# Three parts of x on ScalarE's DMA queue, and a new order in the opening of the first feed-forward block

## The chip, the cores and the metric

The kernel runs on one core of a Trainium2 chip. The metric is the device time of one execution in microseconds (us), the median of several runs; lower is better. The core has a matrix engine (TensorE, PE in the profile, with its weight loads as PEld), VectorE (DVE), ScalarE (ACT), GpSimd (POOL) and SyncE (SP), which here only issues DMAs. The engines run on their own and wait for each other by semaphores; each of them works through its instructions in the order of the program.

## What is computed

Two layers of a decoder trunk on x, 256 tokens by 1024 columns, in float32:

```python
for l in range(DEPTH):
    h = h + 0.5 * swiglu(rms_norm(h, ffn1_norm[l]), ffn1_w_gate[l], ffn1_w_up[l], ffn1_w_down[l])
    h = h + hybrid_mixer(rms_norm(h, mix_norm[l]), w_in[l], ...)
    h = h + 0.5 * swiglu(rms_norm(h, ffn2_norm[l]), ffn2_w_gate[l], ffn2_w_up[l], ffn2_w_down[l])

def swiglu(x, w_gate, w_up, w_down):
    return (jax.nn.silu(x @ w_gate) * (x @ w_up)) @ w_down
```

The change lies in the first feed-forward block of the first layer alone. There `x @ w_gate` and `x @ w_up` have an inner length of 1024 (eight tiles k of 128 rows) and 2816 columns (22 tiles f of 128).

## The kernel before

**Arithmetic.** TensorE multiplies in a reduced format, so every float32 operand is cut into a high and a low part: `wh` is a cast of the weight (a copy on ScalarE or GpSimd), `wl` is the weight minus `wh` (a subtraction on VectorE or GpSimd). The activation has the same two parts, `norm.h` and `norm.l`, which lie side by side as `norm.x`. A "wide" product is `wh` with `norm.x` (512 columns), a "narrow" one `wl` with `norm.h` (256 columns). Each gate or up tile of 128 columns takes eight of each, and `summed` then adds the two halves of the PSUM bank.

**Loads.** `Weights` streams 1 MB pieces into five raw buffers and hands out the split units (`high`, `low`, `take`, `pump`). All loads of weights go through SP. The opening is loaded by hand: `load_x(mp)` brings two of x's eight k tiles (256 KB) into `trunk`; `W.load(i, m)` brings part m of the first gate (i = 0) or up piece (i = 1). In this text x0 to x3 are the four parts of x, g0, g1 and u0, u1 the parts of the gate and up pieces with k tiles 0 and 1, and 2 and 3; g2 and u2 the parts with k tiles 4 to 7 (512 KB each). The next two pieces, for the tiles f of 2 and 3, come behind them. The completion of a DMA counts up one of eight semaphores, DMAHW0 to DMAHW7, which are dealt out in turn over all queues; a DMA that gets a semaphore again waits until the DMA that had it before has landed.

**The opening** (`opening`, and the lines after it up to the loop over f). PE turns x's parts by transposes against `ident` (L535), ScalarE copies the turned part out, scaled (L362, the high part), VectorE makes the low part (L365). With `opening`, the first two tiles f (pairs p0 and p1) are multiplied together, over k tiles 0 to 3 as x and the weights come in, then (`hi`) over k tiles 4 to 7. `warm_up` issues products of ones, whose result nobody reads: WARM ahead of the first transposes, BRIDGE behind them. `norm.sums` and `norm.broadcast` make the reciprocal root that `gated` multiplies in. Then the loop over f takes one gate and one up tile at a time; odd tiles are `swapped` (narrow products first), even ones have the wide products first; from f = 4 on a tile of the down projection (`down`) stands between.

Of the kernel before, what the change touches and what calls it, by code (L numbers as in the profile page):

```python
# [18 lines left out]
P = 128  # L19
S = 256  # L20
D = 1024
KT = D // P
# [131 lines left out]
def kernel(ctx: ExitStack, tc: tile.TileContext, x, ffn1_norm, ffn1_w_gate, ffn1_w_up, ffn1_w_down,  # L154
                      mix_norm, w_in, forget_bias, a_q_norm, a_k_norm, b_q_norm, b_k_norm, c_q_norm, c_k_norm,
                      w_out, ffn2_norm, ffn2_w_gate, ffn2_w_up, ffn2_w_down, const, out):
    nc = tc.nc
# [39 lines left out]
    def tmp(n):  # L197
        return tp.tile([P, 512], F32, name="tmp", tag="tmp")[:, :n]
# [22 lines left out]

    def load_x(mp):
        cols = slice(256 * mp, 256 * mp + 256)
        nc.sync.dma_start(trunk[:, :, cols], x[0].rearrange("(t p) d -> p t d", p=P)[:, :, cols])  # L224

    load_x(0)
    load_gains(rows, ffn1_norm, nc.scalar)
    A.activation(tmp(P), ones, AF.Exp)

    def head_gains(l):  # L230
        gb = at.tile([P, 4, HD], F32, name="gb", tag="sg")
# [7 lines left out]
    def add_ffn(wg, wu, wd, first=False):  # L239
        gsrc, usrc, dsrc = (w.rearrange("(k p) c -> p k c", p=P) for w in (wg, wu, wd))  # L240
        rid = {}

        def half(kind, i):
            j = i // 2
            if (kind, j) not in rid:
                if kind == "d":
                    rid[kind, j] = W.add_raw((2, D), [(np.s_[:], dsrc[:, 2 * j:2 * j + 2, :])])
                else:
                    src = gsrc if kind == "g" else usrc
                    src = src[:, :, 256 * j:256 * j + 256]  # L250
                    cuts = [np.s_[:]]
                    if first and j < 2:
                        cuts = ([np.s_[:, 0:2], np.s_[:, 2:4], np.s_[:, 4:8]],
                                [np.s_[:, :, 0:P], np.s_[:, :, P:2 * P]])[j]
                    rid[kind, j] = W.add_raw((KT, 256), [(c, src[c]) for c in cuts])
            o = i % 2
            if kind == "d":
                W.add_unit(rid[kind, j], lambda r, o=o: r[:, o:o + 1, :], D, 1)
            elif first and j == 0:
                W.add_unit(rid[kind, j], lambda r, o=o: r[:, 4 * o:4 * o + 4], D, 4)  # L260
            else:
                W.add_unit(rid[kind, j], lambda r, o=o: r[:, :, o * P:(o + 1) * P], D, KT)

        for f in range(NF):
            half("g", f)
            half("u", f)
            if f == NF - 1:
                half("d", f - 1 - DOWN_LAG)
            if DOWN_LAG <= f != NF - 2:
                half("d", f - DOWN_LAG)  # L270
        for k in range(NF - DOWN_LAG, NF):
            half("d", k)
# [22 lines left out]
    W.n_raw_done -= RAW_BUFS - 4  # L295
    W.issue()
    for m in range(2):
        if m:
            load_x(m)
        for i in range(2):  # L300
            W.load(i, m)
    for mp in range(2, 4):
        load_x(mp)
    for i in range(2):
        W.load(i, 2)
    load_gains(more_rows[0:16], mix_norm, nc.sync)
    load_gains(more_rows[16:32], ffn2_norm, nc.sync)
    for m in range(2):
# [28 lines left out]
    def mm(o, l, r, start, stop):  # L337
        T.matmul(o, l, r, start=start, stop=stop, skip_group_check=True)  # L338
# [82 lines left out]
    def ffn(norm, nxt, aside=None, first=False):  # L421
# [23 lines left out]
        class Pair:  # L445
# [3 lines left out]
                self.ws = ws or [[[v[:, k] for k in range(KT)] for v in W.take()] for _ in range(2)]  # L449
                self.ps = [bank("gu").rearrange("p (a b) -> p a b", a=2) for _ in range(2)]  # L450

            def wide(self, ks):
                for w, ps in zip(self.ws, self.ps):
                    for k in ks:
                        mm(ps, w[0][k], norm.x[:, k], k == 0, False)

            def narrow(self, ks):
                for w, ps in zip(self.ws, self.ps):
                    for k in ks:
                        mm(ps[:, 0], w[1][k], norm.h[:, k], False, k == KT - 1)  # L460

            def swapped(self, between):

# [6 lines left out]
                        mm(ps, w[0][k], norm.x[:, k], False, k == KT - 1)  # L470
                return self.ps

            def both(self, ks=range(KT)):
                self.wide(ks)
                self.narrow(ks)
                return self.ps

        def summed(ps):

            o = tmp(S)  # L480
            A.copy(o, ps[:, 1])  # L481
            V.tensor_tensor(o, ps[:, 0], o, op=ALU.add)  # L482
            return o
# [24 lines left out]
        def opening():  # L508

            low = [W.high_tiles() for _ in range(2)]  # L510
            p0, p1 = (Pair([[[v[:, k, f * P:(f + 1) * P] for k in range(4)] for v in (h, l)] for _, h, l in low])
                      for f in range(2))

            def split(i, m, high, E):

                src, h, l = low[i]
                ks = slice(2 * m, 2 * m + 2)
                high(h[:, ks], src[:, ks])
                E.tensor_tensor(l[:, ks], src[:, ks], h[:, ks].bitcast(F32), op=ALU.subtract)  # L519

            def wide(i, k):
                for p in (p0, p1):
                    mm(p.ps[i], p.ws[i][0][k], norm.x[:, k], k == 0, False)

            def narrow(i, k):
                for p in (p0, p1):
                    mm(p.ps[i][:, 0], p.ws[i][1][k], norm.h[:, k], False, False)

            def turn(mp):

                ps = []
                for m in (2 * mp, 2 * mp + 1):
                    ps.append(bank("acc")[:, :S])
                    for t in range(2):
                        T.transpose(ps[-1][:, t * P:(t + 1) * P], trunk[:, t, m * P:(m + 1) * P], ident)  # L535
                return ps

            def parts(mp, ps):
                for i in range(2):
                    norm.high(2 * mp + i, ps[i])  # L540
                for i in range(2):
                    norm.low(2 * mp + i, ps[i])

            def squares(c):
                for t in range(2):
                    norm.squares(t, c)

            xT = turn(0)
            warm_up(BRIDGE)
            for m in range(2):  # L550
                ks = (2 * m, 2 * m + 1)
                parts(m, xT)
                split(0, m, G.tensor_copy, V)
                split(1, m, A.copy, G)
                for k in ks:
                    wide(0, k)
                if m:
                    xT = turn(2)
                for k in ks:
                    narrow(0, k)  # L560
                if m:
                    squares(0)
                    parts(2, xT)
                xT = turn(2 * m + 1)
                for k in ks:
                    wide(1, k)
                for k in ks:
                    narrow(1, k)
            parts(3, xT)
            for _ in range(2):  # L570
                W.low_done()
                W.take()
            src, h, _ = W.high_tiles()
            G.tensor_copy(h, src)
            W.high()
            W.low()
            W.low()
            squares(1)
            high = [W.take() for _ in range(2)]
            for f, p in enumerate((p0, p1)):  # L580
                for w, u in zip(p.ws, high):
                    for part, v in zip(w, u):
                        part.extend(v[:, k, f * P:(f + 1) * P] for k in range(4))
            return p0, p1

        lo, hi = range(KT // 2), range(KT // 2, KT)
        if first:
            p0, p1 = opening()
# [5 lines left out]
            p1.both(lo)  # L594
        W.pump()
        norm.sums()
        (g0, u0), (g1, u1) = p0.both(hi), p1.ps
        W.pump()
        g0, u0 = summed(g0), summed(u0)
        W.pump()  # L600
        p1.wide(hi)
        norm.broadcast(first)
        p1.narrow(hi)
        W.pump()
        t_, th = gated(g0)
        if not first:
# [4 lines left out]
        for f in range(1, NF):  # L611
            last = f == NF - 1
            def lagging():
                if DOWN_LAG <= f != NF - 2:
                    down(f - DOWN_LAG - last)

            if f == 1:
                g, u = g1, u1
            elif f % 2:
                g, u = Pair().swapped(lagging)  # L620
            else:
                p = Pair()
                p.wide(range(KT))
                lagging()
                p.narrow(range(KT))
                g, u = p.ps
            if last:
                W.pump()
            low_first = first and f == 1
            g = summed(g)  # L630
            if low_first:
                W.low()
            if not last:
                u = summed(u)
            t_, th = gated(g)
            if last:
                W.low()
                down(f - DOWN_LAG)
            else:
                if low_first:  # L640
                    W.high()
                else:
                    W.pump()
                if f == 1:
                    lagging()
                if f >= DOWN_LAG:
                    W.pump()
            silu(t_, th)
            hidden(f, t_, th, summed(u) if last else u, 3 if last else 1 + (first and f in (2, 3)))
            if f == 4 and first:  # L650
                load_small()
            if f == 8 and aside:
                aside()
# [653 lines left out]
```

## Time and profile before

| what | value |
|---|---|
| median of 3 runs | 1009.53 us (1009.43 to 1010.38) |
| the profiled execution, its own time | 1009.91 us |
| its span (first to last instruction) | 1008.2 us |
| PE busy in the span | 1003.4 us (100%), 5724 matmuls |
| PEld, DVE, ACT, POOL busy | 857.9, 795.3, 588.2, 169.1 us |
| HBM traffic | 184 MB, 182 GB/s over the span |

A matmul's busy time contains the time in the pipeline, so rows of products that follow each other overlap: 16 wide products on end take 3.82 us, though each lasts 390 ns. The pace of a row of products is what counts, and a busy PE is not a sign of full pace.

### The profile page before, as it was taken

To read this page: it belongs to the slowest core of one execution; us is meant where nothing else is said; L and a number is where in the kernel's file an instruction comes from. 1 tells how busy PE (TensorE), PEld (TensorE's weight loads), DVE (VectorE), ACT (ScalarE), POOL (GpSimd) and SP (SyncE) were. 2 spreads that over 40 slices of the span, in tenths; PEclk is the share of its full clock that TensorE was granted. 3 is DMA by queue.
4 is the path that set the end of the run, shared out by engine and by line. 5 is a ranking of instruction groups with operands and counts; after the bars stand their busy time and mean duration, and the time that the engine had idled before them with its cause. 6 is when DMAs were issued, how large, how long until landed. Compare 5 with 4: busy or idle time off the path is not lost.

```text
span 1008.2 us, 15271 instructions
## 1 busy us (share of the span) xinstructions
PE 1003.4 (100%) x5724; PEld 857.9 (85%) x5724; DVE 795.3 (79%) x1466; ACT 588.2 (58%) x1078; POOL 169.1 (17%) x196
## 2 busy tenths in 40 slices
PE   9999999999999999999999999999999999999998
PEld 7888888888878888888888888888888788888887
DVE  5978778779988877777878777787899877777775
ACT  6555555567776555555465555556677765555552
POOL 2003000058732000000000030001776320000000
PEclk9999999999999999999999999999999999999999
DMA  9765647474624455655655655665556255474731
GB/s 287 265 215 165 224 153 238 138 244 168 225 89 168 149 185 170 206 181 202 203 168 172 209 185 190 201 192 176 180 205 230 68 180 172 130 244 136 242 126 42
DMA packets 133497, 184.60 MB, mean 183 GB/s; under 512 B 7152, under 2 KB 106928, under 8 KB 133424
## 3 DMA queue, kind: packets, MB, share of 16 engines
q1 hardware_dynamic: 133392, 183.62, 54.8%
q8 instruction: 45, 0.74, 0.3%
q14 instruction: 28, 0.23, 0.1%
q10 hardware_dynamic: 32, 0.01, 0.0%
HBM read 182.55 MB, written 1.06 MB: 182 GB/s over the span
## 4 chain that ended last, share of the span: by engine, by line
PE 98%; DMA 1%; SPq 0%; ACT 0%; issue 0%; DVE 0%
PE ps_gu L338 66%; PE ps_acc L338 30%; PE ps_acc L179 1%; PE ps_acc L373 1%; DMA raw<-in_ffn_w_up_dram 1%; PE ps_gu L179 1%; SPq L99 0%; SPq L224 0%; PE ps_acc L940 0%; ACT wh L125 0%; PE ps_acc L400 0%; PE ps_acc L875 0%; PE ps_acc L821 0%; DVE trunk L417 0%; PE ps_acc L402 0%
## 5 line engine op out<-in xcount | busy, mean ns | idle before, releaser
L129 DVE TENSOR_TENSOR wl<-raw,wh 128x1024 fp32r<-128x1024 f32 (+2 forms) x342 | 418.2, 1232 | 25.4 <-ACT wh L125 25.0
L125 ACT CAST wh<-raw 128x1024 fp32r<-128x1024 f32 (+2 forms) x341 | 342.2, 1036 | 24.3 <-PE ps_gu L338 13.9
L338 PE MATMUL ps_gu<-xhl,wh 128*128 128x512 f32 x1408 | 330.5, 390 | 0.5 <-ACT wh L125 0.5
L338 PEld LDWEIGHTS ps_gu<-xhl,wh 128*128 128x128 f32 x1408 | 262.7, 188 | 54.8 <-ACT wh L125 0.9
L338 PEld LDWEIGHTS ps_gu<-xhl,wl 128*128 128x128 f32 x1408 | 175.9, 191 | 4.1 <-DVE wl L519 0.2
L338 PE MATMUL ps_gu<-xhl,wl 128*128 128x256 f32 x1408 | 178.7, 283 | 0.0
L482 DVE TENSOR_TENSOR tmp<-ps_gu,tmp 128x256 f32<-128x256 f32 x176 | 72.9, 423 | 109.3 <-ACT tmp L481 108.8
L338 PE MATMUL ps_gu<-wh,xhl 128*128 128x512 f32 (+2 forms) x512 | 155.1, 378 | 0.0
L338 PE MATMUL ps_acc<-wh,hh 128*128 128x512 f32 (+1 forms) x352 | 137.2, 390 | 0.0
L338 PE MATMUL ps_acc<-wl,hh 128*128 128x512 f32 (+1 forms) x352 | 137.0, 389 | 0.0
L338 PE MATMUL ps_acc<-wh,hl 128*128 128x512 f32 (+1 forms) x352 | 136.5, 388 | 0.0
L481 ACT COPY tmp<-ps_gu 128x256 f32<-128x256 f32 x176 | 63.4, 371 | 92.1 <-PE ps_gu L338 91.9
L338 PEld LDWEIGHTS ps_gu<-wh,xhl 128*128 128x128 f32 x512 | 94.6, 188 | 16.8 <-issue 1.7
L496 ACT CAST hh<-tmp 128x256 fp32r<-128x256 f32 x80 | 32.6, 407 | 120.2 <-DVE tmp L493 120.2
L338 PE MATMUL ps_gu<-wl,xhl 128*128 128x512 f32 (+2 forms) x256 | 95.7, 374 | 0.0
L488 ACT ACTIVATE tmp<-tmp 128x256 f32<-128x256 f32 x88 | 36.9, 419 | 82.9 <-DVE tmp L486 82.8
L349 POOL TENSOR_TENSOR y_n<-msq,minus_half 128x2 f32<-128x2 f32 x6 | 7.0, 1174 | 440.9 <-DVE msq L348 440.9
L338 PEld LDWEIGHTS ps_acc<-wh,hl 128*128 128x128 f32 x352 | 66.1, 188 | 13.8
L338 PEld LDWEIGHTS ps_acc<-wh,hh 128*128 128x128 f32 x352 | 66.2, 188 | 12.6
L338 PEld LDWEIGHTS ps_acc<-wl,hh 128*128 128x128 f32 x352 | 66.3, 188 | 12.3 <-DVE wl L129 0.2
L338 PEld LDWEIGHTS ps_gu<-wl,xhl 128*128 128x128 f32 x256 | 48.2, 188 | 7.0
L493 DVE TENSOR_TENSOR tmp<-tmp 128x256 f32<-128x256 f32 x88 | 37.6, 427 | 3.0
(228 smaller groups left out, 903.7 us busy)
## 6 DMA issues: line engine op xcount, KB each, us to landing
raw<-in_ffn_w_down_dram SPq DMA_DIRECT2D x44, 1024.0 KB, 5.0
raw<-in_ffn_w_gate_dram SPq DMA_DIRECT2D x42, 1024.0 KB, 7.0
raw<-in_ffn_w_up_dram SPq DMA_DIRECT2D x42, 1024.0 KB, 7.9
raw<-in_w_in_dram SPq DMA_DIRECT2D x24, 1024.0 KB, 5.0
raw<-in_w_out_dram SPq DMA_DIRECT2D x8, 1024.0 KB, 5.0
raw<-in_w_in_dram SPq DMA_DIRECT2D x4, 768.0 KB, 4.8
raw<-in_w_in_dram SPq DMA_DIRECT2D x4, 656.0 KB, 4.0
raw<-in_ffn_w_gate_dram SPq DMA_DIRECT2D x3, 512.0 KB, 7.9
```

Of the source, the lines that this page charges most:

```text
L125: self.nc.scalar.copy(hv, src)
L129: (engine or self.nc.vector).tensor_tensor(lv, self.srcs[self.n_low], hv.bitcast(F32), op=ALU.subtract)
L179: T.transpose(b[:, 64 * i:64 * i + 64], src[r], ident[r, r])
L338: T.matmul(o, l, r, start=start, stop=stop, skip_group_check=True)
L349: G.tensor_tensor(y, dst, minus_half[:, :n], op=ALU.pow)
L373: T.transpose(ps[:, i, t * P:(t + 1) * P], trunk[:, t, (2 * mp + i) * P:(2 * mp + i + 1) * P], ident)
L481: A.copy(o, ps[:, 1])
L482: V.tensor_tensor(o, ps[:, 0], o, op=ALU.add)
L488: A.activation(th, t_, AF.Tanh, scale=0.5)
L493: V.tensor_tensor(t_, u, t_, op=ALU.mult)
L496: (V.tensor_copy if late else A.copy)(hh, t_)
```

## The change

It has six parts, all of them in the first feed-forward block of the first layer.

1. `load_x` issues x1, x2 and x3 on ScalarE's queue, and a loop right behind ScalarE's first activation calls it for these three. The call for x1 between the weights is taken out; the old loop for x2 and x3 below stays, so that these two are loaded a second time, to the same place, and on ScalarE's queue too.
2. g2 and u2 are cut into two parts of 256 KB each (here g2a, g2b, u2a, u2b).
3. GpSimd casts g2 in two halves, ScalarE u2 in two halves.
4. Over k tiles 4 to 7, the wide gate products of p0 and p1 stand first, then p0's narrow gate products and its up products; p1's narrow gate products come next.
5. Tile f = 3 has its wide products first.
6. For f = 1, both sums (`summed`) stand ahead of a low part (`W.low`).

```diff
 def load_x(mp):
-        nc.sync.dma_start(trunk[:, :, cols], x[0].rearrange("(t p) d -> p t d", p=P)[:, :, cols])
+        (nc.scalar if mp else nc.sync).dma_start(trunk[:, :, cols], x[0].rearrange("(t p) d -> p t d", p=P)[:, :, cols])

     load_x(0)
     load_gains(rows, ffn1_norm, nc.scalar)
     A.activation(tmp(P), ones, AF.Exp)
+    for mp in range(1, 4):
+        load_x(mp)
...
-                        cuts = ([np.s_[:, 0:2], np.s_[:, 2:4], np.s_[:, 4:8]],
+                        cuts = ([np.s_[:, 0:2], np.s_[:, 2:4], np.s_[:, 4:6], np.s_[:, 6:8]],
...
     for m in range(2):
-        if m:
-            load_x(m)
         for i in range(2):
             W.load(i, m)
     for mp in range(2, 4):
         load_x(mp)
     for i in range(2):
-        W.load(i, 2)
+        for m in (2, 3):
+            W.load(i, m)
...
-            src, h, _ = W.high_tiles()
-            G.tensor_copy(h, src)
-            W.high()
+            for copy in (G.tensor_copy, A.copy):
+                src, h, _ = W.high_tiles()
+                for ks in (slice(0, 2), slice(2, 4)):
+                    copy(h[:, ks], src[:, ks])
...
-        (g0, u0), (g1, u1) = p0.both(hi), p1.ps
+        if first:
+            p0.wide(hi, (0,))
+            p1.wide(hi, (0,))
+            p0.narrow(hi, (0,))
+            p0.both(hi, (1,))
+        else:
+            p0.both(hi)
+        (g0, u0), (g1, u1) = p0.ps, p1.ps
...
-        p1.wide(hi)
+        if first:
+            p1.narrow(hi, (0,))
+        p1.wide(hi, (1,) if first else (0, 1))
         norm.broadcast(first)
-        p1.narrow(hi)
+        p1.narrow(hi, (1,) if first else (0, 1))
...
-            elif f % 2:
+            elif f % 2 and not (first and f == 3):
                 g, u = Pair().swapped(lagging)
...
             g = summed(g)
+            if not last:
+                u = summed(u)
             if low_first:
                 W.low()
-            if not last:
-                u = summed(u)
```

Three places show how this moves the instructions. The first is ScalarE from the start of the program, before; tmp<-in_ffn_norm is the load of the gains, xhl the turned x, wh<-raw 128x512 the cast of u0:

```order
L208 DMA tmp<-in_ffn_norm_dram 16x128
L228 ACT_TABLE_LOAD
L228 ACTIVATE tmp<-ones 128x128 [waits Pool_49]
L362 ACTIVATE xhl<-ps_acc,gT 128x256 [waits DVE_49,PE_49]
L362 ACTIVATE xhl<-ps_acc,gT 128x256 [waits PE_49]
L518 CAST wh<-raw 128x512 [waits DMAHW3_49]
```

and the same place now:

```order
L208 DMA tmp<-in_ffn_norm_dram 16x128
L228 ACT_TABLE_LOAD
L228 ACTIVATE tmp<-ones 128x128 [waits Pool_49]
L224 DMA trunk<-in_x_dram 128x2x256 x2
L224 DMA trunk<-in_x_dram 128x2x256 [waits DMAHW0_49]
L224 DMA trunk<-in_x_dram 128x2x256 [waits DMAHW6_49,DMAHW3_49]
L224 DMA trunk<-in_x_dram 128x2x256 [waits DMAHW5_49,DMAHW0_49]
L363 ACTIVATE xhl<-ps_acc,gT 128x256 [waits DVE_49,PE_49]
L363 ACTIVATE xhl<-ps_acc,gT 128x256 [waits PE_49]
L518 CAST wh<-raw 128x512
```

Five loads of x (x1, x2, x3, and x2 and x3 again) now stand ahead of the first copy of the turned x. Counted in turn, DMAHW0 belongs first to the gains and then to x3, DMAHW3 to u0, DMAHW5 to g1, DMAHW6 to x2.

The second place is SP's queue from the start, before:

```order
L224 DMA trunk<-in_x_dram 128x2x256
L99 DMA raw<-in_ffn_w_gate_dram 128x2x256
L99 DMA raw<-in_ffn_w_up_dram 128x2x256
L224 DMA trunk<-in_x_dram 128x2x256
L99 DMA raw<-in_ffn_w_gate_dram 128x2x256
L99 DMA raw<-in_ffn_w_up_dram 128x2x256
L224 DMA trunk<-in_x_dram 128x2x256
L224 DMA trunk<-in_x_dram 128x2x256 [waits DMAHW0_49]
L99 DMA raw<-in_ffn_w_gate_dram 128x4x256 [waits DMAHW1_49]
L99 DMA raw<-in_ffn_w_up_dram 128x4x256 [waits DMAHW2_49]
```

and now:

```order
L224 DMA trunk<-in_x_dram 128x2x256
L99 DMA raw<-in_ffn_w_gate_dram 128x2x256
L99 DMA raw<-in_ffn_w_up_dram 128x2x256
L99 DMA raw<-in_ffn_w_gate_dram 128x2x256
L99 DMA raw<-in_ffn_w_up_dram 128x2x256
L99 DMA raw<-in_ffn_w_gate_dram 128x2x256 [waits DMAHW1_49]
L99 DMA raw<-in_ffn_w_gate_dram 128x2x256 [waits DMAHW2_49]
L99 DMA raw<-in_ffn_w_up_dram 128x2x256 [waits DMAHW4_49]
L99 DMA raw<-in_ffn_w_up_dram 128x2x256 [waits DMAHW6_49]
```

g1 and u1 stand one place earlier; u2a waits for x1 (DMAHW4) and u2b for x2 (DMAHW6).

The third place is TensorE over k tiles 4 to 7, before; gate banks are 158 (p0) and 160 (p1), up banks 159 and 161:

```order
L338 MATMUL ps_gu_158<-xhl_149,wh_249 128x512 x4
L338 MATMUL ps_gu_159<-xhl_149,wh_252 128x512 x4
L338 MATMUL ps_gu_158<-xhl_149,wl_250 128x256 x4
L338 MATMUL ps_gu_159<-xhl_149,wl_253 128x256 x4
L338 MATMUL ps_gu_160<-xhl_149,wh_249 128x512 x4
L338 MATMUL ps_gu_161<-xhl_149,wh_252 128x512 x4
```

and now, with gate banks 162 and 164, up banks 163 and 165:

```order
L339 MATMUL ps_gu_162<-xhl_153,wh_253 128x512 x4
L339 MATMUL ps_gu_164<-xhl_153,wh_253 128x512 x4
L339 MATMUL ps_gu_162<-xhl_153,wl_254 128x256 x4
L339 MATMUL ps_gu_163<-xhl_153,wh_257 128x512 x4
L339 MATMUL ps_gu_163<-xhl_153,wl_258 128x256 x4
L339 MATMUL ps_gu_164<-xhl_153,wl_254 128x256 x4
L339 MATMUL ps_gu_165<-xhl_153,wh_257 128x512 x4
```

The first product with the up weights (wh_252 before, wh_257 now) stands behind twelve products instead of four.

## Rows read from the trace of the kernel before

**Rows 1.** Four stretches: busy us of each engine, granted clock (PEclk), DMA share.

```profile
0.00:5.00 5.00, 3.95 (x17) 3.69 (x18) 0.17 (x1) 1.75 (x3) 1.12 (x8) 1.00 0.54 168
5.00:20.50 15.50, 14.81 (x87) 12.08 (x86) 10.13 (x18) 11.50 (x25) 5.30 (x6) 1.00 1.07 308
20.50:100.00 79.50, 79.50 (x428) 68.91 (x427) 66.11 (x114) 44.59 (x77) 7.86 (x14) 1.00 0.69 225
100.00:1008.20 908.20, 905.12 (x5198) 773.19 (x5197) 718.85 (x1335) 530.33 (x976) 154.80 (x169) 1.00 0.53 177
```

**Rows 2.** TensorE's longest waits in the whole span: total us, times, longest.

```profile
PE ps_gu L338 <- POOL minus_half L218: 1.0, 1, 1.0
PE ps_gu L338 <- ACT wh L125: 0.5, 1, 0.5
```

**Rows 3.** TensorE's timeline in the opening: start, us, line, operation, count.

```profile
1.05 2.93 PE L338 MATMUL ps_gu<-ones 128*128 128x128 f32 x12 [1.05 <-POOL minus_half L218]
...
4.12 1.11 PE L535 MATMUL ps_acc<-ident,trunk 128*128 128x128 f32 x4
5.03 0.92 PE L338 MATMUL ps_gu<-ones 128*128 128x128 f32 x6
5.98 1.17 PE L338 MATMUL ps_gu<-xhl,wh 128*128 128x512 f32 x4
...
10.67 0.60 PE L535 MATMUL ps_acc<-ident,trunk 128*128 128x128 f32 x4
...
15.20 1.21 PE L338 MATMUL ps_gu<-xhl,wh 128*128 128x512 f32 x4 [0.46 <-ACT wh L125]
...
20.58 3.82 PE L338 MATMUL ps_gu<-xhl,wh 128*128 128x512 f32 x16
24.24 3.99 PE L338 MATMUL ps_gu<-xhl,wl 128*128 128x256 f32 x32
```

**Rows 4.** ScalarE's timeline from the start.

```profile
0.79 0.46 ACTq L208 DMA_DIRECT2D tmp<-in_ffn_norm_dram  x1
1.27 1.28 ACT L228 ACT_TABLE_LOAD   x1 [1.27 <-PEq L1295]
2.57 0.31 ACT L228 ACTIVATE tmp<-ones 128x128 f32<-128x128 f32 x1
4.84 0.90 ACT L362 ACTIVATE xhl<-ps_acc,gT 128x256 fp32r<-128x256 f32 x2 [1.97 <-PE ps_acc L535]
...
14.10 1.05 ACT L125 CAST wh<-raw 128x1024 fp32r<-128x1024 f32 x1 [1.27 <-DMA raw<-in_ffn_w_up_dram]
```

**Rows 5.** SP's longest wait in the first 70 us: total us, times, longest.

```profile
SPq L99 <- DVE wl L129: 25.0, 6, 11.7
```

**Rows 6.** SP's issues at the start: start, us.

```profile
0.79 0.44 SPq L224 DMA_DIRECT2D trunk<-in_x_dram  x1
...
2.81 0.47 SPq L99 DMA_DIRECT2D raw<-in_ffn_w_gate_dram  x1
...
3.83 0.98 SPq L224 DMA_DIRECT2D trunk<-in_x_dram  x2
4.86 0.47 SPq L99 DMA_DIRECT2D raw<-in_ffn_w_gate_dram  x1
```

**Rows 7.** DMAs x2, x3 and g2, last field: us from issue to landing.

```profile
trunk<-in_x_dram SPq DMA_DIRECT2D x1, 256.0 KB, 6.3
...
trunk<-in_x_dram SPq DMA_DIRECT2D x1, 256.0 KB, 6.6
...
raw<-in_ffn_w_gate_dram SPq DMA_DIRECT2D x1, 512.0 KB, 7.5
```

**Rows 8.** VectorE's timeline around the sums of tile f = 1.

```profile
25.06 0.42 DVE L482 TENSOR_TENSOR tmp<-ps_gu,tmp 128x256 f32<-128x256 f32 x1
25.40 1.21 DVE L129 TENSOR_TENSOR wl<-raw,wh 128x1024 fp32r<-128x1024 f32 x1
26.53 0.42 DVE L482 TENSOR_TENSOR tmp<-ps_gu,tmp 128x256 f32<-128x256 f32 x1
```

More of the change, by code (lines that the diff above doesn't have):

```diff
@@ L450, in __init__, with wide, narrow @@
                 self.ps = [bank("gu").rearrange("p (a b) -> p a b", a=2) for _ in range(2)]
-            def wide(self, ks):
-                for w, ps in zip(self.ws, self.ps):
+            def wide(self, ks, which=(0, 1)):
+                for i in which:
                     for k in ks:
-                        mm(ps, w[0][k], norm.x[:, k], k == 0, False)
-            def narrow(self, ks):
-                for w, ps in zip(self.ws, self.ps):
+                        mm(self.ps[i], self.ws[i][0][k], norm.x[:, k], k == 0, False)
+            def narrow(self, ks, which=(0, 1)):
+                for i in which:
                     for k in ks:
-                        mm(ps[:, 0], w[1][k], norm.h[:, k], False, k == KT - 1)
+                        mm(self.ps[i][:, 0], self.ws[i][1][k], norm.h[:, k], False, k == KT - 1)
             def swapped(self, between):
@@ L471, in swapped, with both @@
                 return self.ps
[L473 to L476, printed above, removed]
+            def both(self, ks=range(KT), which=(0, 1)):
+                self.wide(ks, which)
+                self.narrow(ks, which)
         def summed(ps):
```

## The prediction

> **What bounds the kernel now.** I read the stretches of the span first. From 20.5 us to 100 us TensorE is busy in all of its 79.50 us, and in the 908.2 us behind them in 905.12 [rows 1]; of its waits in the whole span, only the one at the start and 0.5 us for a cast of up weights reach half a microsecond [rows 2]. So behind the opening there is no gap that a change could close and none that could take up a delay: whatever the opening gains or loses stands in the end time, one for one. The change touches nothing but the opening and the tiles f up to 3. What counts is when TensorE begins with tile f = 2, at 20.58 us [rows 3].
>
> The opening of before runs from its first wide product at 5.98 us to 20.58 us [rows 3], 14.6 us. The work in it, at the pace of rows without a wait: 16 wide products take 3.82 us with the last one's 0.39, so (3.82 - 0.39) / 15 = 0.229 us apiece; 32 narrow ones 3.99 us, 0.120 apiece; four transposes 0.60 us on end, about 0.11 apiece [rows 3]. 32 wide, 32 narrow and 12 transposes make 7.3 + 3.8 + 1.3, with some 0.6 us (an estimate) for the broadcast 13.1 us. Thus 1.5 us of the 14.6 are waits, the largest ahead of 15.20, where the cast of u2 began at 14.10 because its load came late [rows 3, 4]. These 1.5 us are all that the change can win.
>
> **What the change does, part by part.**
>
> *x on ScalarE's queue.* This is the part that decides. Before, ScalarE issues the gains at 0.79, loads its table, is done with the exponential at 2.88, and stands idle until its first copy of turned x at 4.84 [rows 4]. Now five issues stand between, and an engine works in order: SP's queue shows what a wait at an issue does, since SP stood 25.0 us on six of them in the first 70 us with everything behind them [rows 5]. Each issue costs 0.46 to 0.47 us [rows 4, 6]. x1, x2 and x3 go out at about 2.9, 3.4 and 3.9 us: the gains, for which x3 waits, are needed by then anyway. That would end at 4.4, hidden under the idle time. But the second x2 has to wait until the first has landed, since it writes the same place, and until u0 has; the second x3 until the first x3 and g1 have. ScalarE's first copy of turned x, the casts of u0, u1, u2 and all sums of squares are queued behind that, and VectorE's low parts and TensorE's first wide product hang on the first copy.
>
> When do the first x3 and g1 land? Seven parts of 256 KB must be in: x0, g0, u0, g1 on SP and x1, x2, x3 on ScalarE. Before, the seventh part in line was x2, issued at 3.83 and landed 6.3 later, at 10.1; the eighth, x3, was issued 0.5 later and landed 6.6 after that, at 10.95 [rows 6, 7]. I take 10.5, between the two, because u1 is in flight beside x3. The early bound: x0 issued at 0.79 is in at about 3.8 (estimate: TensorE turns it at 4.12 [rows 3]), and six more parts of 262 kB at the 308 GB/s of the stretch from 5 to 20.5 us [rows 1] make 6 x 0.85 = 5.1 us: 8.9. The late bound: x3 comes in only when all that SP can have in flight is in, g2's size of data too, which before landed at 4.86 + 7.5 = 12.4 [rows 6, 7].
>
> No row shows two loaded queues side by side. The Trainium skill (DMA: Bandwidth & Descriptors, Queues, rings and completion order) says that each DMA engine takes turns between the queues, a packet at a time. By that x3 would land with about three parts of SP's queue beside it, which is the middle of my range, and neither bound; by that page the sum would stay as it is.
>
> So the issue of the second x3 begins at 10.5, ends at 11.0, and the first copy begins at 11.0 instead of 4.84: 6.2 us later, with 4.6 and 8.0 for the bounds (9.4 and 12.85).
>
> *What the delay gives back.* At 11.0 every weight of k tiles 0 to 3 is in, and GpSimd has cast g0. From there the opening is limited by TensorE's own pace, so the 1.5 us of waits go: 6.2 - 1.5 = 4.7 us. What must be hidden for that: ScalarE's copies, casts and squares up to k tile 7, about 6 us by rows like those shown, against some 7 us that TensorE needs for k tiles 0 to 3; it is near but holds, as do the second loads of x2 and x3 (issued before 11.0, needed some 4 us later; at 0.85 us a part two are in within that). If one of them were late, it would be by a fraction of a microsecond, which the range holds.
>
> *TensorE's pace after the pause.* TensorE ends the BRIDGE products at 5.95 and now has nothing until about 12.1, a pause of 6 us. The granted clock in the rows is 1.00, that is 2.4 GHz, everywhere [rows 1], but the durations at the start of the span say otherwise: the four transposes at 4.12 took 1.11 us on end, those at 10.67 took 0.60 [rows 3]; between the ends of two of them that is about 0.23 and 0.11 us, the one twice the other. So the work that followed the pause ahead of the span went at half pace, from 1.05 until about 5. If the pause of 6 us has the same consequence, and as much work goes at half pace, TensorE loses half of those 4 us, 2.0 us, and nothing hides them, because it is then the engine that everybody waits for. The bounds are 0 (no fall) and 3.5 (all of the work on k tiles 0 to 3, 7 us at full pace, at half for twice as long as I take).
>
> The Trainium skill (TensorE: Matmul & The Clock Gate, Part 1) says the clock falls to 1.2 GHz when the engine has been idle and returns after sustained work. By that page this term is there; without it the sum would be 2.0 us less. The duration of the first transposes agrees with it, the clock of the rows does not show it.
>
> *g2 and u2 in two parts, cast by halves.* The same bytes and the same columns; two more issues on SP (0.47 each) and two more instructions on GpSimd and ScalarE. The issues wait for x1 and x2 on the other queue, but all four are out by about 10.6, and the first product with g2 now comes at about 21, with u2 at 23. Nothing of it is on the path: 0, and the same for u1 and g1 a place earlier.
>
> *The 0.5 MB loaded twice* is 1.7 us of DMA time at 308 GB/s [rows 1]; it pushes the next two pieces back by that, but they are needed 6 us later: 0.
>
> *Gate products first* would hide the wait for u2's cast at 15.20 (0.46 to 0.7 us); that wait is gone anyway and is in the 1.5 us already.
>
> *f = 3 with its wide products first, both sums ahead of the low part.* The sums of f = 1 free the two banks that f = 3 needs. Before they end at 25.5 and 26.95, the low part of 1.2 us between them [rows 8], and f = 3's gate products begin at 26.1, the up products about 1 us later [rows 3]. Now both sums end before the low part, and the up bank is needed 1.8 us (eight wide products) after the gate bank. But ScalarE and VectorE run closer behind TensorE than before, since both have the opening's work in a shorter time. I count 0.1 us, between 0 and 0.6.
>
> **Sum.** 6.2 - 1.5 + 2.0 + 0.1 = 6.8 us on the profiled execution's 1009.91 us, whose span is 1008.2: 1016.7. The median of the three runs is 0.4 us below that execution, so 1016.3 us.
>
> **Rivals.**
> - *The pause costs no pace* (the clock rows, 1.00 throughout [rows 1], speak for it; the first transposes against): 1014.3. Chance 0.15.
> - *ScalarE's queue is served last*, x3 in at 12.4 (before, parts came in by order of issue, and SP has issued more by then): 8.0 - 1.5 + 2.0 + 0.1, at 1018.1. Chance 0.08.
> - *ScalarE is not held.* If the wait at an issue held only the DMA, or x3 came in far sooner, ScalarE would start at 4.84 and x would come in beside the weights: up to 1.5 us of waits gone, I take 1.0, and 1008.5. The point from which it decides is a first copy at 4.84 + 1.5 = 6.3 us. Against it: seven parts can't be in by then, when even the early bound has the last at 8.9, and SP's waits [rows 5] hold all that follows. Chance 0.04.
> - *Held only for some 3 us*, no loss of pace, the opening's waits gone: within 0.2%. It needs x3 in by about 8, ahead of my early bound. Chance 0.03.
>
> **How the numbers follow.** The forecast (held to about 11, loss of pace) has 0.70. The range goes from the early bound with no loss, 4.6 - 1.5 = 3.1, at 1012.6, to the late bound with a larger loss (8.0 - 1.5 + 3.5), at 1019.5. A measurement of this kernel can tell about 0.2%, or 2 us, from no change: slower by more than that 0.93, within it 0.03, faster 0.04.
>
> **What would show it.** In the profile after: ScalarE's queue with five loads of x, the last near 10.5, and the first copy of turned x at 11; a gap of TensorE of about 6 us ahead of its first wide product near 12; the first wide products further apart than 0.229 us; tile f = 2 near 27.3 instead of 20.58, and every later stretch as before. It is wrong if ScalarE's copies start near 5, if TensorE has a second gap of over 1 us (then a chain I called hidden isn't), or if the time beyond 30 us has changed.

## The result, and the profile after

The changed kernel takes 1017.1 us (median of four runs, 1016.37 to 1017.38) where the kernel before, run beside it, takes 1009.76: a ratio of 1.0074, with an interval of 1.0061 to 1.0086. It is slower by 7.3 us, 6.2 to 8.7 by that interval. The profiled execution shown here took 1017.03 us, with a span of 1015.3 against 1008.2.

The stretches come first, as in [rows 1]. The columns are the stretch, its length, the busy time of TensorE, its weight loads, VectorE, ScalarE and GpSimd, the granted clock, the DMA share and GB/s. After:

```profile
5.00:12.00 7.00, 1.77 (x9) 1.50 (x8) 0.88 (x3) 1.35 (x3) 0.61 (x1) 1.00 1.06 341
12.00:28.50 16.50, 16.50 (x84) 14.23 (x85) 10.91 (x18) 11.48 (x25) 6.84 (x6) 1.00 1.10 323
28.50:107.00 78.50, 78.50 (x423) 68.19 (x422) 64.16 (x112) 43.54 (x74) 7.60 (x14) 1.00 0.60 198
107.00:1015.30 908.30, 904.91 (x5198) 773.08 (x5196) 718.74 (x1335) 530.77 (x976) 153.59 (x169) 1.00 0.53 177
```

The last 908.30 us hold 5198 matmuls and 904.91 us of work; before, the last 908.20 us held 5198 and 905.12 [rows 1]. In the stretch ahead of them TensorE has no gap in either kernel. All but a few tenths of a microsecond of what changed lies ahead of 28.5 us. There, between 5 and 12 us, TensorE is busy for 1.77 us of 7, while the DMA engines move 341 GB/s: it has nothing to do, although data comes in at no lower a rate than in the stretches beside it. TensorE's waits name the gap (total us, times, longest), in place of those of [rows 2]:

```profile
PE ps_gu L339 <- DVE xhl L366: 5.2, 1, 5.2
PE ps_gu L339 <- POOL minus_half L218: 1.0, 1, 1.0
```

One wait of 5.2 us on `xhl`, the first k tile of x, is new; the wait for the cast of up weights is gone. Who is behind it is told by ScalarE's timeline (start, us, engine, line, operation, idle time before and its releaser), to be held against [rows 4]:

```profile
1.28 1.28 ACT L228 ACT_TABLE_LOAD   x1 [1.28 <-PEq L1305]
1.35 0.98 ACTq L224 DMA_DIRECT2D trunk<-in_x_dram  x2
2.58 0.31 ACT L228 ACTIVATE tmp<-ones 128x128 f32<-128x128 f32 x1
3.40 7.10 ACTq L224 DMA_DIRECT2D trunk<-in_x_dram  x3
10.61 0.84 ACT L363 ACTIVATE xhl<-ps_acc,gT 128x256 fp32r<-128x256 f32 x2 [7.72 <-DMA trunk<-in_x_dram]
```

"ACTq" is the engine's queue of DMA issues. The row that starts at 3.40 holds three issues and lasts 7.10 us, up to 10.50: the first x3, then the second x2 and x3, which stand until the places that they write have been filled once. The first copy of turned x, at 4.84 before [rows 4], begins at 10.61, and its releaser is a DMA of x, not the transposes for which it waited before. The chain of waits (start, us, what) gives the same in order of time:

```profile
3.40 6.71 DMA trunk<-in_x_dram
...
10.13 0.38 ACTq L224
...
10.61 0.48 ACT xhl L363
...
11.12 0.49 DVE xhl L366
...
11.75 2.90 PE ps_gu L339 x8
```

The first x3, issued at 3.40, is in at 10.11. The last issue follows, then ScalarE's copy, VectorE's remainder and TensorE's first wide product at 11.75. From the landing to that product nothing waits for anything else. TensorE's timeline, to be held against [rows 3]:

```profile
5.03 1.49 PE L339 MATMUL ps_gu<-ones 128*128 128x128 f32 x6
11.75 2.05 PE L339 MATMUL ps_gu<-xhl,wh 128*128 128x512 f32 x4 [5.23 <-DVE xhl L366]
...
14.45 1.06 PE L535 MATMUL ps_acc<-ident,trunk 128*128 128x128 f32 x4
...
18.53 0.60 PE L535 MATMUL ps_acc<-ident,trunk 128*128 128x128 f32 x4
...
27.46 3.80 PE L339 MATMUL ps_gu<-xhl,wh 128*128 128x512 f32 x16
31.09 2.08 PE L339 MATMUL ps_gu<-xhl,wl 128*128 128x256 f32 x16
33.01 3.82 PE L339 MATMUL ps_gu<-xhl,wh 128*128 128x512 f32 x16
```

The first four wide products fill 11.75 to 13.59, where the next group begins, 0.46 us apiece; those of tile f = 2 fill 27.46 to 31.09, 3.63 / 16 = 0.227 apiece. Four transposes take 1.06 us at 14.45 and 0.60 at 18.53. So TensorE goes at half pace for some 5 us behind the pause, up to about 17 us. Tile f = 2 begins at 27.46 instead of 20.58 [rows 3], 6.9 us later, and f = 3 at 33.01 without a wait.

### The profile page after: what moved, and what is told of

It is laid out like the page before. It is cut to its first block, busy times and chain, and to the rows that moved or that the text cites. A ratio compares the mean times of both kernels' runs of the same rounds, so it can differ in the third digit from the quotient of the medians.

```text
span 1015.3 us, 15280 instructions
## 1 busy us (share of the span) xinstructions
PE 1005.6 (99%) x5724; PEld 860.7 (85%) x5724; DVE 794.9 (78%) x1466; ACT 588.7 (58%) x1079; POOL 169.4 (17%) x197
## 3 DMA queue, kind: packets, MB, share of 16 engines
HBM read 183.08 MB, written 1.06 MB: 181 GB/s over the span
## 4 chain that ended last, share of the span: by engine, by line
PE 99%; DMA 1%; DVE 0%; ACT 0%; ACTq 0%; issue 0%
PE ps_gu L339 66%; PE ps_acc L339 29%; PE ps_acc L179 1%; PE ps_acc L374 1%; DMA trunk<-in_x_dram 1%; PE ps_gu L179 1%; DMA tmp<-in_ffn_norm_dram 0%; PE ps_acc L535 0%; PE ps_acc L950 0%; PE ps_acc L401 0%; DVE xhl L366 0%; ACT xhl L363 0%; PE ps_acc L831 0%; PE ps_acc L885 0%; DVE trunk L418 0%; ACTq L224 0%
## 5 line engine op out<-in xcount | busy, mean ns | idle before, releaser
L363 ACT ACTIVATE xhl<-ps_acc,gT 128x256 fp32r<-128x256 f32 x48 | 19.1, 474 | 39.6 <-PE ps_acc L374 27.4
```

The source lines that it names most:

```text
L363: A.activation(self.h[:, m], src, AF.Copy, scale=gT[:, self.col + m:self.col + m + 1])
```

## The experiments

In the order in which they tell the parts apart. Differences are against the kernel before, run in the same session.

**The second loads alone, on the kernel before.** Everything stays as it was, except that x2 and x3 are loaded a second time by ScalarE.

```diff
-    def load_x(mp):
+    def load_x(mp, eng=nc.sync):
...
+    for mp in range(2, 4):
+        load_x(mp, nc.scalar)
```

> The kernel before with nothing added but the second loads of x2 and x3 on ScalarE's queue, ahead of its first copy; the first loads stay on SP. Theory: x3, the eighth part on SP, lands near 10.9 us as in the kernel before, so ScalarE's first copy starts near 11.4 us, TensorE pauses and is slow afterwards: 6.6 us of delay, 1.0 to 1.5 us of waits gone, 2 to 2.5 us for the pace, 1016.5 to 1018 us, as much as the whole change. Rival (the first loads on ScalarE's queue, the cuts or the new order cost the time): 1009 to 1011 us.

1017.51 us against 1009.16, a ratio of 1.0082 (1.0066 to 1.0097). ScalarE's and TensorE's timelines:

```profile
10.18 1.15 ACTq L224 DMA_DIRECT2D trunk<-in_x_dram  x2
11.44 0.84 ACT L364 ACTIVATE xhl<-ps_acc,gT 128x256 fp32r<-128x256 f32 x2 [8.56 <-DMA trunk<-in_x_dram]
```

```profile
12.58 2.04 PE L340 MATMUL ps_gu<-xhl,wh 128*128 128x512 f32 x4 [6.22 <-DVE xhl L367]
```

The whole loss is there with nothing but these two DMAs. By the medians it is even 1.0 us larger than the change's 7.3, with intervals that overlap, and the first copy is 0.8 us later than after the change (11.44 against 10.61): here the first x3 lands at 10.86, after the change, with x on ScalarE's queue, at 10.11.

**The change without the second loads.** The old loop over x2 and x3 is taken out, so that each part of x is loaded once.

```diff
-    for mp in range(2, 4):
-        load_x(mp)
```

> The changed kernel with every part of x loaded once: the old loop for x2 and x3 is taken out, all else stays. Theory (ScalarE is held by the issues of the second loads): the first copy of turned x starts near 4.9 us instead of 10.6, TensorE has no pause of 5 us and no slow products behind it, tile f = 2 starts between 19.1 and 20.6 us, and the time is between 1008.0 and 1009.8 us, at or below the kernel before. Rival (the two queues side by side or the new order cost the time): it stays at 1014 us or above.

1009.78 us against 1009.16, a ratio of 1.0008 (0.9999 to 1.0017). The first copy of x is back at 4.85 and the pause is gone, with 0.6 us that can't be told from none: the time is within what was expected, but not at or below the kernel before. So the loss hangs on the second loads, and the rest of the change brings nothing that these runs can tell. ScalarE and GpSimd show a small loss that was not in the prediction:

```profile
1.35 0.98 ACTq L224 DMA_DIRECT2D trunk<-in_x_dram  x2
...
4.85 0.90 ACT L361 ACTIVATE xhl<-ps_acc,gT 128x256 fp32r<-128x256 f32 x2 [1.97 <-PE ps_acc L533]
7.59 0.62 ACT L516 CAST wh<-raw 128x512 fp32r<-128x512 f32 x1 [1.84 <-DMA raw<-in_ffn_w_up_dram]
```

```profile
5.80 0.61 POOL L516 CAST wh<-raw 128x512 fp32r<-128x512 f32 x1 [4.42 <-DMA raw<-in_ffn_w_gate_dram]
```

x1 and x2 go out at 1.35, beside g0 and u0 on the other queue, which land later: the cast of u0 waits 1.84 us for its load, the cast of g0 begins at 5.80, and the first wide product stands at 6.47 instead of 5.98 [rows 3].

**x on ScalarE's queue alone**, on the kernel before, each part loaded once.

```diff
-        nc.sync.dma_start(trunk[:, :, cols], ...)
+        (nc.scalar if mp else nc.sync).dma_start(trunk[:, :, cols], ...)
...
+    for mp in range(1, 4):
+        load_x(mp)
...
-        if m:
-            load_x(m)
...
-    for mp in range(2, 4):
-        load_x(mp)
```

> The kernel before with only x1, x2 and x3 moved to ScalarE's queue, each loaded once. Theory (the queue itself costs nothing like 7 us, but x1 and x2, issued during the table load, come in ahead of g0 and u0): GpSimd's cast of g0 starts at 5.8 instead of 4.63 and ScalarE's cast of u0 at 7.6 instead of 5.94 us, the first wide product near 6.5 instead of 5.98; tile f = 2 at 20.3 to 21.2; within 0.7 us of the kernel before. Rival (loads on ScalarE's queue slow the opening): slower than before by over 2 us.

1009.85 us against 1009.21, a ratio of 1.0006 (0.9997 to 1.0015): no difference that can be told. The cast of g0 stands at 5.84 and the first wide product at 6.50, as in the run above, so the later weights come from the move of x and not from the halves. Tile f = 2 begins at 20.28: the half microsecond is regained in the opening, where the wait ahead of u2's products [rows 3] is gone.

**One second load instead of two.** x2 is loaded twice, x3 once. ScalarE then waits for the first x2 instead of the first x3, which comes in earlier.

```diff
     for mp in range(2, 4):
-        load_x(mp)
+    load_x(2)
```

> The changed kernel with x2 loaded twice but x3 once, so that ScalarE is held until x2 (and u0) are in, not x3. Theory: a shorter hold, the first copy near 8.5 us, about 2 us ahead of the changed kernel's 10.6; tile f = 2 about 2 us earlier than 27.5, or 3 to 4 us if the shorter pause spares TensorE the slow products; 1013.0 to 1015.5 us. Rival (the 0.5 MB of extra traffic costs the time): half of the extra bytes gone, so half of the 7.3 us, 1013.5, but with the first copy still at 4.9 us; the place of the first copy tells the two apart.

1014.19 us against 1009.16, a ratio of 1.0049 (1.0035 to 1.0062). ScalarE, then TensorE's granted clock by stretches of a microsecond (columns as at the top):

```profile
3.13 5.39 ACTq L224 DMA_DIRECT2D trunk<-in_x_dram  x2
8.63 0.84 ACT L362 ACTIVATE xhl<-ps_acc,gT 128x256 fp32r<-128x256 f32 x2 [5.75 <-DMA trunk<-in_x_dram]
```

```profile
9.00:10.00 1.00, 0.23 (x1) 0.27 (x2) 0.86 (x3) 0.97 (x3) 0.00 (x0) 0.77 1.10 350
...
11.00:12.00 1.00, 1.00 (x4) 0.81 (x4) 0.00 (x0) 0.00 (x0) 1.00 (x2) 0.50 1.10 348
12.00:13.00 1.00, 1.00 (x7) 1.00 (x6) 0.00 (x0) 0.00 (x0) 0.30 (x1) 0.53 1.11 335
13.00:14.00 1.00, 1.00 (x7) 0.86 (x6) 0.37 (x1) 0.88 (x3) 0.00 (x0) 1.00 1.17 301
```

```profile
9.77 2.04 PE L338 MATMUL ps_gu<-xhl,wh 128*128 128x512 f32 x4 [3.38 <-DVE xhl L365]
```

The first copy moves from 10.61 to 8.63, 2.0 us. The time moves by 2.3 us, from a loss of 7.3 to one of 5.0, each against the kernel before beside it (by 2.9 between the two medians, which come from two sessions). The delay follows the landing for which the last issue waits. The clock rows of this execution show what those of after did not: 0.50, the 1.2 GHz level, in the work that follows the pause (four wide products at 9.77 take 2.04 us), and 1.00 from 13 us on.

**TensorE kept busy through the pause.** BRIDGE, the number of rounds of products with ones ahead of the first wide product, goes from 3 to 22; all else is as after the change.

```diff
-BRIDGE = 3
+BRIDGE = 22
```

> The changed kernel with 22 instead of 3 products of ones behind the first transposes, so that TensorE is busy through most of ScalarE's hold; the result of these products isn't read. Theory (TensorE's pace falls over the pause): the first wide products come 0.23 us apart instead of 0.46, tile f = 2 starts 2.0 to 2.6 us earlier than 27.5, and the time is 1014.5 to 1015.2 us. Rival (the slow pace comes from elsewhere, as from the loads, or costs nothing since ScalarE is what limits): the time stays at 1016.5 to 1017.5 us.

1015.12 us against 1009.16, a ratio of 1.0060 (1.0047 to 1.0074). TensorE's timeline:

```profile
5.03 5.72 PE L339 MATMUL ps_gu<-ones 128*128 128x128 f32 x44
11.62 1.17 PE L339 MATMUL ps_gu<-xhl,wh 128*128 128x512 f32 x4 [0.87 <-DVE xhl L366]
...
24.77 3.59 PE L339 MATMUL ps_gu<-xhl,wh 128*128 128x512 f32 x15
```

The first wide product stands where it stood after (11.62 against 11.75), but from there it takes 24.77 - 11.62 = 13.15 us to tile f = 2, where after takes 27.46 - 11.75 = 15.71. That difference, 2.6 us, is the price of the lower pace in the traces; the spans differ by 1015.3 - 1012.6 = 2.7. By the medians it is less, 2.0 us between the two medians and 1.4 by the two ratios, with intervals that overlap: this kernel's four runs lie between 1014.41 and 1016.92, and the profiled one is the fastest of them. The pace is shown; its price in the time is known to about a microsecond.

**The second loads issued by SP.** As after the change, but the second x2 and x3 go through SP's queue.

```diff
-        (nc.scalar if mp else nc.sync).dma_start(trunk[:, :, cols], ...)
+        (nc.scalar if mp and not again else nc.sync).dma_start(trunk[:, :, cols], ...)
...
-        load_x(mp)
+        load_x(mp, True)
```

> The changed kernel with the second loads of x2 and x3 issued by SP instead of ScalarE, at the same place in the program: the same bytes twice, the same waits for the first loads, but another engine stands at them. Theory (the price is that ScalarE stands): the first copy starts near 4.9 us; SP stands until x3 is in, so g2 and u2 come later, by 3 to 5 us, and TensorE has a wait of 1 to 4 us ahead of k tiles 4 to 7; 1010 to 1013 us. Rival (the extra 0.5 MB or the wait as such costs it, wherever it stands): 1016 to 1018 us.

1013.47 us against 1009.21, a ratio of 1.0042 (1.0028 to 1.0055); half a microsecond above the end of what was expected. ScalarE is free, as expected, and SP stands instead; but the one wait of 1 to 4 us that was expected of TensorE came as several small ones. ScalarE's first copy, then SP's queue of issues:

```profile
4.54 0.84 ACT L363 ACTIVATE xhl<-ps_acc,gT 128x256 fp32r<-128x256 f32 x2 [1.66 <-PE ps_acc L535]
```

```profile
8.18 2.37 SPq L224 DMA_DIRECT2D trunk<-in_x_dram  x2
10.60 0.97 SPq L99 DMA_DIRECT2D raw<-in_ffn_w_gate_dram  x2
11.62 0.98 SPq L99 DMA_DIRECT2D raw<-in_ffn_w_up_dram  x2
```

The wait has only changed its engine. The same two loads now hold g2 and u2, which go out at 10.60 and 11.62 instead of 3.92 and 6.45 after, and TensorE gets its waits in small pieces instead of one:

```profile
16.26 1.66 PE L339 MATMUL ps_gu<-xhl,wh 128*128 128x512 f32 x6 [0.75 <-POOL wh L576]
...
22.53 3.91 PE L339 MATMUL ps_gu<-xhl,wh 128*128 128x512 f32 x16 [0.26 <-DVE tmp L482]
...
29.14 3.92 PE L339 MATMUL ps_gu<-xhl,wh 128*128 128x512 f32 x16 [0.80 <-DVE tmp L482]
```

Only 2.0 us of the loss are there when f = 2 begins, at 22.53; the rest comes behind it, as at 29.14, where f = 3 waits for VectorE's sums. Followed back, the chain of that wait begins with a load of up weights, which SP issued at 17.11 and which landed at 25.08; the same load was issued at 13.15 in the kernel with x loaded by SP, further below. So the hold moved SP's whole line of loads by about 4 us. SP has no arithmetic behind its issues, and without a long pause TensorE kept its pace (its first four wide products, at 6.17, take 1.20 us against 2.05 after the change), so the same wait cost 4.3 us there instead of 7.3.

**The other parts without the move of x.** After the change, with x loaded by SP as before: u2 and g2 in two parts, casts by halves, gate products first, and the new order of f = 3.

```diff
-        (nc.scalar if mp else nc.sync).dma_start(trunk[:, :, cols], ...)
+        nc.sync.dma_start(trunk[:, :, cols], ...)
...
-    for mp in range(1, 4):
-        load_x(mp)
...
+        if m:
+            load_x(m)
```

> The changed kernel without its first part: all parts of x once and on SP in their old places; the cuts, the casts by halves, gate products first, the new order of f = 3 and of the sums stay. Theory: these are worth only waits of the opening, at most the 1.5 us and mostly the 0.5 to 0.7 us ahead of 15.20 us; tile f = 2 starts at 19.6 to 20.4 instead of 20.58, and the time is 0.2 to 1.0 us below the kernel before. Rival (part of the delay of the changed kernel comes from these parts): slower than before by over 0.5 us.

1009.27 us against 1009.21, a ratio of 1.0002 (0.9993 to 1.0011). The gain that I expected is not in the time. In the profile it is there up to f = 2, which begins at 19.80 without the wait of [rows 3]:

```profile
19.80 3.82 PE L339 MATMUL ps_gu<-xhl,wh 128*128 128x512 f32 x16
```

How much the opening differs between executions, and where the gain goes, is what the next two are for.

**The kernel before, once more**, unchanged.

> The kernel before once more, unchanged, for a second profile beside the next one. In its first profile tile f = 2 starts at 20.58 us, but its runs on this chip are 0.4 to 0.7 us below that execution. If the moment at which TensorE's pace rises at the start differs between executions, the opening ends at another time than 20.58, by up to 1 us, with the same waits for the loads; rival: the same 20.58 to within 0.1.

1009.52 us over eight runs. In its profile f = 2 begins at 20.16 instead of 20.58, and the wait ahead of u2's products is 0.40 us. So 0.4 us of the start of f = 2 is the difference between two executions of one kernel:

```profile
7.54 0.66 PE L535 MATMUL ps_acc<-ident,trunk 128*128 128x128 f32 x4
...
20.16 3.81 PE L338 MATMUL ps_gu<-xhl,wh 128*128 128x512 f32 x16
```

Some 0.3 us of it is a load: the transposes of x1 stand at 7.54 here, and in the first profile at 7.86, where they waited 0.20 us for x. It is not TensorE's pace at the start, as I had supposed: the products with ones at 5.03 took longer here (1.25 us against 0.92 [rows 3]), and the opening still ended earlier.

**The other parts, once more**, the kernel with x loaded by SP as before.

> The changed kernel without its first part once more: its first profile has tile f = 2 at 19.80, 0.78 us ahead of the kernel before, but its median is that of the kernel before. If the difference is in the pace at the start, this profile and that of the kernel before next to it differ in the opening by no more than their times do, 0 to 0.4 us; rival: f = 2 again 0.7 to 0.8 us ahead, with the time lost behind it.

1009.75 us over eight runs against 1009.47, a ratio of 1.0000 (0.9989 to 1.0011). In this profile f = 2 begins still earlier, at 19.64, 0.5 us ahead of the kernel before beside it, but the time is no shorter: nearer to the rival, time lost behind f = 2, than to the pace at the start. TensorE's timeline in this profile, then VectorE's, first in the earlier profile of this kernel, then in this one:

```profile
19.64 3.82 PE L339 MATMUL ps_gu<-xhl,wh 128*128 128x512 f32 x16
...
25.45 3.93 PE L339 MATMUL ps_gu<-xhl,wh 128*128 128x512 f32 x16
```

```profile
16.29 1.23 DVE L129 TENSOR_TENSOR wl<-raw,wh 128x1024 fp32r<-128x1024 f32 x1
...
24.19 0.75 DVE L482 TENSOR_TENSOR tmp<-ps_gu,tmp 128x256 f32<-128x256 f32 x2
```

```profile
16.91 1.23 DVE L129 TENSOR_TENSOR wl<-raw,wh 128x1024 fp32r<-128x1024 f32 x1 [0.69 <-ACT wh L125]
...
24.98 0.75 DVE L482 TENSOR_TENSOR tmp<-ps_gu,tmp 128x256 f32<-128x256 f32 x2
```

TensorE is 0.16 us earlier in the second, but VectorE's low part at 16.91 waits for a cast by ScalarE, and the sums of f = 1 are 0.8 us later, about where they stood before [rows 8]. These sums free the banks of f = 3, which so begins at 25.45, 0.2 us behind the end of f = 2; further small gaps follow. The first transposes of the next layer norm show the total: they stand at 188.11 in the earlier profile and at 188.91 in this one, with 188.95 and 188.58 in the two profiles of before. From the start of f = 2 it is 168.31 us in the earlier and 169.27 in this one (168.37 and 168.42 in before's), so 0.96 us was lost behind f = 2. VectorE is not the start of this. ScalarE's casts, in the earlier profile and in this one, wait for a load of gate weights:

```profile
18.64 1.05 ACT L125 CAST wh<-raw 128x1024 fp32r<-128x1024 f32 x1 [0.21 <-DMA raw<-in_ffn_w_gate_dram]
```

```profile
19.38 1.05 ACT L125 CAST wh<-raw 128x1024 fp32r<-128x1024 f32 x1 [0.17 <-DMA raw<-in_ffn_w_gate_dram]
```

SP issued this load at 10.88 in the earlier profile and at 11.69 in this one, and the chain of waits leads from its landing at 19.36 over this cast and VectorE's low part and sums to the products at 25.45. So the gain was given back to a weight load that came 0.7 to 0.8 us later. Whether anything of it remains on average is below what these runs tell.

## Where the prediction was right and where not

It named 1016.3 us within 1012.6 to 1019.5, and slower; 1017.1 was measured. Its steps:

- **ScalarE held at the second loads: right.** The last issue was forecast near 10.5 and stands at 10.13; the first copy was forecast at 11.0 and came at 10.61. The term was 6.2 and is 10.61 - 4.84 = 5.8 us. The two second loads alone give the whole loss, and without them it is gone. The rival in which ScalarE is not held fell with the copy's releaser; the one that has ScalarE's queue served last fell with the landing at 10.11 instead of 12.4. From 5 to 6 us SP's queue moved 146 packets and ScalarE's 140, from 6 to 10 us 1047 and 418. The Trainium skill (DMA: Bandwidth & Descriptors, Queues, rings and completion order) says that each DMA engine takes turns between the queues; the first of these microseconds agrees, and equal turns over the whole load are not shown.
- **The times of the issues: wrong, with little consequence.** x1 and x2 were to go out at 2.9 and 3.4, behind the table load and the exponential. They went out at 1.35, while the table was loading. What the step missed is that they are then under way together with g0 and u0, whose casts came 1.2 to 1.7 us later where x was loaded once; with the hold in place nobody waited for that. x3 went out at 3.40 instead of 3.9 and landed 0.4 us ahead of the forecast; how far the one made the other is not shown.
- **The opening's waits given back: right.** At full pace, with TensorE kept busy, the opening took 13.15 us where 13.1 was forecast, so the 14.6 of before lose 1.45 (forecast 1.5). In the other profile of before the opening took 20.16 - 6.03 = 14.1 us, so this term is known to some 0.4 us.
- **TensorE's pace: right in kind, too small in the trace.** Forecast 2.0 with a bound of 3.5; the traces have 15.71 - 13.15 = 2.6. I took the work after the pause to be as much as that at the start of the span; it was some 5 us at half pace instead of 4. The bound of 3.5 doesn't follow from its words: 7 us of work at full pace lose 7 at half pace, and 3.5 is what 7 us spent at half pace lose. By the medians it lies between 1.4 and 2.0. The rival without this term would need first products 0.23 us apart, and they were 0.46.
- **f = 3's banks: right.** 0.1 was forecast; there is no wait at 33.01. The halves, the gate products first and the second loads' traffic cost nothing on the path, as forecast.
- **The sum.** 5.8 - 1.5 + 2.6 = 6.9 us in the trace, which is how much later f = 2 begins (27.46 - 20.58); forecast 6.8, at 27.3. The profiled executions differ by 7.1, the medians by 7.3. The hold was taken 0.4 too large and the pace 0.6 too small, so a part of the close result is that the two cancel, which is luck; and against the other profile of before, f = 2 begins 7.3 us later and not 6.9.
- **"Whatever the opening gains or loses stands in the end time": right for this loss, not for a gain.** After, the 6.9 us stand behind 28.5 us to within some 0.2 us. With the second loads on SP, the 2.0 us at f = 2 grew to 4.3, since SP's later loads were late too. Of a gain of 0.4 to 0.9 us in the opening (19.80 and 19.64 against 20.58 and 20.16), one execution gave all back to the chain from a later weight load to VectorE's sums. A stretch in which TensorE never waits says that nobody is late at its present start. It doesn't say by how much it could start earlier.

What stays open: whether the halves and the new order are worth some tenths of a microsecond on average, the exact price of the lower pace, and in what measure the two queues shared the DMA engines.

## What to carry to other kernels

A second load into the same place waits for the first, and it waits at the head of the issuing engine's queue, so its price is not its bytes but everything that is queued behind it on that engine. When a load is moved to another engine, look for the line that it leaves behind, and let no issue that can wait stand ahead of arithmetic that others need. A pause of TensorE cost more here than its length, since the work behind it was slower for some 5 us; and to read what an earlier start would be worth, ask which engine or load would be late next.

## What the runs showed of the hardware

- **ScalarE issues DMAs while it loads its activation table.** The two issues at 1.35 lie within the load from 1.28 to 2.56, in after and in all runs with x on ScalarE's queue. An issue that waits, though, holds the arithmetic behind it, after the change to 10.61.
- **The clock rows can miss a low clock.** After's profile has 1.00 in every stretch with first products 0.46 us apart; the run with one second load shows 0.50, the 1.2 GHz level, for the same spacing (2.04 us for four). The durations tell in both. The Trainium skill (TensorE: Matmul & The Clock Gate, Part 1) says that the clock falls when the engine has been idle and that clock records are not always to be trusted; these rows agree with both.
- **At the start of the span the pace rises at another moment in each execution.** Six products with ones at 5.03 took 0.92 us before [rows 3], 1.49 after and in the run with x loaded once, and 1.25 in the kernel before once more. The start of f = 2 doesn't follow it: in the kernel before it is 20.58 with 0.92 and 20.16 with 1.25. What this spread is worth in the time is not shown.
